# A feed-forward in a fixed order: the output weights' transfers take places further ahead in the transfer queue

## The chip, the cores and the metric

The kernel runs on one core of one Trainium2 chip. The metric is the device time of one execution in microseconds, median of several runs; the kernel before takes 1002.35 us (three runs: 1003.61, 1000.15 and 1002.35).

In the profile, PE is the matrix engine (TensorE) and PEld its weight loads, DVE is VectorE, ACT is ScalarE, POOL is GpSimd, and SP is the engine that issues nearly all transfers. Each of them takes its own instructions in order and waits at semaphores for the others.

## The reference

Two residual layers over a sequence of 512 frames of width 1024, in float32. Layer 0 mixes by pooling, layer 1 by chunked attention; each is followed by the same gated feed-forward with 2816 hidden channels, which is where the change lies:

```python
def conv_ffn(h, w_gate, w_val, conv_w, conv_b, w_out):
    a = h @ w_gate
    ap = jnp.pad(a, ((0, 0), (CONV_W - 1, 0), (0, 0)))
    a = ap[:, 0:S] * conv_w[0] + ap[:, 1:S + 1] * conv_w[1] + ap[:, 2:S + 2] * conv_w[2] + conv_b
    return (jax.nn.silu(a) * (h @ w_val)) @ w_out

for i in range(DEPTH):            # DEPTH = 2
    ...                           # pooling mixer or chunked attention, residual
    h = rmsnorm(x, ffn_norm[i])
    x = x + conv_ffn(h, ffn_w_gate[i], ffn_w_val[i], ffn_conv_w[i], ffn_conv_b[i], ffn_w_out[i])
```

## The kernel before

**Precision.** Every factor of a product is split in a high part and a low part (hi and lo), and a product is three matmuls: hi by hi, lo by hi, hi by lo (function `mm3`, lines 123 to 125). For a weight this means: a transfer brings the raw block, ACT copies it to hi with rounding (line 409), and DVE subtracts hi from raw to get lo (line 410). Tiles are named so in the trace: `wo_r` is a raw block of the out weights, `ow_h` and `ow_l` its two parts; `gv_r` is a raw block of the gate or value weights, `g_h` and `g_l` its parts.

**The hidden blocks.** The 2816 hidden channels are 22 blocks of 128 (f = 0 to 21). A block takes two raw weight blocks of 512 KB, gate and value. From block 5 on they go through seven smaller products with sums of weights (`sa`, `sb`) before them and sums of results behind them; from block 8 on, these are the "wide" form of lines 610 and 612, in the banks `st_m`, `st_b` and `st_t`. ACT copies the first state of the bank `st_m` to the tile `v` (line 619) before PE may go on into that bank. The steps of three neighbouring blocks are interleaved by a table written out by hand, `PLACES`, and from block 8 to the end of the table the order in which DVE, ACT and SP get their instructions is the order of the code. PE's order is that of the code throughout.

**The out product.** The 22 blocks form four groups of 5, 6, 6 and 5 (`OUT`). When a group's hidden blocks are finished, the generator `output(g)` works it into the residual stream: for each of 8 row blocks d of the result it needs the weights of (g, d), 320 or 384 KB, and makes one `mm3` for each hidden block of the group, which PE runs between the products of the next group's hidden blocks. The loop at the end of `ffn` pulls from the generator with `next(queue[0])`, one matmul at a time, at a rate worked out from `points`, `WAIT` and `HOLD`. So while the hidden blocks of group 1 are computed, PE works off the out product of group 0, and so on; that of group 3 comes alone at the end.

**Buffers of the out weights.** For groups 0 to 2 the raw block goes to a buffer of its own (`tag="or"`) in a pool with one buffer for each name, so the transfer of a row block can start only when DVE has made the lo part of the row block before it. The hi and lo parts have two buffers each. For group 3 the raw blocks share the three buffers of the gate and value weights.

**Order around the change.** `load(d + 1)` issues the transfer and, right behind it, the hi part at the start of row block d; the lo part follows two `mm3` later (line 810). SP issues transfers in the order of the code, and one that waits for its buffer holds up all behind it.

## Time and profile before

| | |
|---|---|
| runs | 1003.61, 1000.15, 1002.35 us; median 1002.35 us |
| the profiled execution | 1003.79 us, of which the span of its instructions is 1001.9 us |
| PE busy | 972.8 us, 97% of the span |
| DVE busy | 804.4 us, 80% |
| ACT busy | 572.5 us, 57% |
| POOL busy | 103.2 us, 10% |
| transfers | 102.83 MB, mean 103 GB/s |
| mean granted clock of PE | 0.994 |

Times in the profile count from the start of the span. The feed-forward of layer 0 lies at about 45 to 385 us, attention follows, and the feed-forward of layer 1 begins at about 640 us and ends the kernel. The part in which the order of DVE, ACT and SP is that of the code lies at about 131 to 345 us in layer 0 and 733 to 965 us in layer 1. A matmul's record is about 0.39 us long, but the next one starts 0.23 us after it: records of neighbours overlap. In a list of waits, "A <- B: x, n, y" says that A's engine sat idle for x us in total before A, n times, the longest y, until B. In a timeline the last bracket is the idle time before an instruction and what ended it.

### The profile page before, as it was taken

To read this page: it belongs to the slowest core of one execution; us is meant where nothing else is said; L and a number is where in the kernel's file an instruction comes from. 1 tells how busy PE (TensorE), PEld (TensorE's weight loads), DVE (VectorE), ACT (ScalarE), POOL (GpSimd) and SP (SyncE) were. 2 spreads that over 40 slices of the span, in tenths; PEclk is the share of its full clock that TensorE was granted. 3 is DMA by queue.
4 is the path that set the end of the run, shared out by engine and by line. 5 is a ranking of instruction groups with operands and counts; after the bars stand their busy time and mean duration, and the time that the engine had idled before them with its cause. 6 is when DMAs were issued, how large, how long until landed. Compare 5 with 4: busy or idle time off the path is not lost.

```text
span 1001.9 us, 13807 instructions
## 1 busy us (share of the span) xinstructions
PE 972.8 (97%) x5038; PEld 821.5 (82%) x5038; DVE 804.4 (80%) x1452; ACT 572.5 (57%) x990; POOL 103.2 (10%) x90
## 2 busy tenths in 40 slices
PE   9999999899989999999999999999999889989998
PEld 8788988788868888888888787888988778778886
DVE  8999889889879855442786888999989787889953
ACT  7665555546446444345898887565555444446521
POOL 2300000000000013204435441000000000000000
PEclk9999999999999999999999999999999999999999
DMA  8222232232223224232443342332322323232323
GB/s 332 92 76 86 90 111 94 93 115 75 85 106 116 71 82 146 88 122 85 123 117 93 91 119 75 100 110 70 112 91 75 116 74 101 89 116 74 101 83 112
DMA packets 37428, 102.83 MB, mean 103 GB/s; under 512 B 4432, under 2 KB 7904, under 8 KB 37360
## 3 DMA queue, kind: packets, MB, share of 16 engines
q1 hardware_dynamic: 37296, 101.90, 30.9%
q8 instruction: 40, 0.66, 0.3%
q14 instruction: 28, 0.23, 0.1%
q0 software_dynamic: 32, 0.04, 0.0%
q10 hardware_dynamic: 32, 0.00, 0.0%
HBM read 95.60 MB, written 2.14 MB: 98 GB/s over the span
## 4 chain that ended last, share of the span: by engine, by line
PE 64%; DVE 21%; DMA 7%; ACT 4%; issue 3%; SPq 0%; DVEq 0%; ACTq 0%
DMA wo_r<-wout 7%; PE out L124 5%; PE out L125 5%; PE out L123 5%; PE st_m L610 4%; PE gv L124 3%; PE gv L125 3%; PE gv L123 3%; PE qk L124 3%; PE qk L123 3%; PE qk L125 3%; DVE g_l L410 3%; PE st_m L612 2%; DVE ow_l L410 2%; PE st_t L610 2%
## 5 line engine op out<-in xcount | busy, mean ns | idle before, releaser
L409 ACT ACTIVATE ow_h<-wo_r 128x640 fp32r<-128x640 f32 (+1 forms) x64 | 50.6, 790 | 124.7 <-DMA wo_r<-wout 83.1
L125 PE MATMUL out<-one,ow_l 128*128 128x512 f32 x224 | 88.4, 395 | 3.6 <-DVE ow_l L410 3.6
L123 PE MATMUL out<-one,ow_h 128*128 128x512 f32 x224 | 88.5, 395 | 0.0
L124 PE MATMUL out<-one,ow_h 128*128 128x512 f32 x224 | 88.4, 395 | 0.0
L610 PE MATMUL st_m<-two,g_h 128*128 128x512 f32 x224 | 72.4, 405 | 14.6 <-ACT v L619 14.5
L817 DVE TENSOR_TENSOR X<-out,X 128x512 f32<-128x512 f32 (+1 forms) x65 | 43.9, 677 | 42.0 <-PE out L125 41.9
L610 PE MATMUL st_m<-h,g_h 128*128 128x512 f32 x224 | 70.5, 396 | 0.0
L610 PEld LDWEIGHTS st_m<-two,g_h 128*128 128x128 f32 x224 | 40.3, 189 | 28.7 <-ACT v L619 20.2
L424 DVE SCALAR_TENSOR_TENSOR c<-a,col,c 128x511 f32<-128x511 f32 (+1 forms) x76 | 56.1, 741 | 3.2 <-ACT c L421 3.2
L410 DVE TENSOR_TENSOR ow_l<-wo_r,ow_h 128x640 fp32r<-128x640 f32 (+1 forms) x64 | 56.4, 882 | 2.4 <-ACT ow_h L409 2.4
L125 PEld LDWEIGHTS out<-one,ow_l 128*128 128x128 f32 x224 | 42.5, 190 | 10.9 <-DVE ow_l L410 4.5
L125 PE MATMUL qk<-wqk_h,two 128*128 128x512 f32 x128 | 51.4, 402 | 0.0
L610 PEld LDWEIGHTS st_m<-h,g_h 128*128 128x128 f32 x224 | 42.8, 191 | 9.8
L123 PE MATMUL qk<-wqk_h,two 128*128 128x512 f32 x128 | 50.8, 409 | 0.0
L124 PE MATMUL qk<-wqk_l,two 128*128 128x512 f32 x128 | 50.8, 397 | 0.0
L612 PEld LDWEIGHTS st_m<-two,g_l 128*128 128x128 f32 x224 | 42.7, 191 | 9.4
L123 PEld LDWEIGHTS out<-one,ow_h 128*128 128x128 f32 x224 | 42.8, 191 | 6.1
L124 PEld LDWEIGHTS out<-one,ow_h 128*128 128x128 f32 x224 | 42.6, 190 | 6.3 <-DVE one L435 0.3
L1047 DVE CUSTOM_DVE_ANT_0 sb<-sc,B 128x128 f32<-128x128 f32 (+1 forms) x64 | 31.1, 485 | 18.9 <-PE sc L1044 18.1
L612 PE MATMUL st_m<-h,g_l 128*128 128x256 f32 x224 | 45.5, 285 | 0.0
L421 ACT ACTIVATE c<-a,col 128x512 f32<-128x512 f32 x38 | 30.6, 810 | 26.0 <-DVE a L768 24.6
L612 PE MATMUL st_m<-two,g_l 128*128 128x256 f32 x224 | 44.8, 282 | 0.0
(378 smaller groups left out, 2966.8 us busy)
## 6 DMA issues: line engine op xcount, KB each, us to landing
gv_r<-gv SPq DMA_DIRECT2D x86, 512.0 KB, 3.7
wo_r<-wout SPq DMA_DIRECT2D x32, 384.0 KB, 4.5
wo_r<-wout SPq DMA_DIRECT2D x32, 320.0 KB, 2.9
wqk_r<-wqk SPq DMA_DIRECT2D x16, 512.0 KB, 3.4
wv_r<-wv SPq DMA_DIRECT2D x8, 512.0 KB, 3.4
wo_r<-wo SPq DMA_DIRECT2D x8, 512.0 KB, 3.4
xt<-xt SPq DMA_DIRECT2D x4, 512.0 KB, 5.4
X<-xT SPq DMA_DIRECT2D x8, 256.0 KB, 7.5
```

What stands on the lines that cost most here:

```text
L123: yield nc.tensor.matmul(o, sh, mh, start=first, stop=False, **how)
L124: yield nc.tensor.matmul(o, sh, ml, start=False, stop=False, **how)
L125: yield nc.tensor.matmul(o, sl, mh, start=False, stop=last, **how)
L409: nc.scalar.activation(hi[:, :n], raw[:, :n], AF.Copy)
L410: return hi, lo, lambda: nc.vector.tensor_sub(lo[:, :n], raw[:, :n], hi[:, :n].bitcast(F32))
L421: nc.scalar.activation(c, a, AF.Identity, scale=cw[2], bias=cw[3])
L424: nc.vector.scalar_tensor_tensor(c[:, j:], a[:, :S - j], cw[2 - j], c[:, j:], op0=OP.mult, op1=OP.add)
L610: nc.tensor.matmul(o, hi[:, c], B[i, name], start=first and i == 0, stop=False, **how)
L612: nc.tensor.matmul(o[:, 0], lo[:, c], B[i, name][:, 0], start=False, stop=i == 3, **how)
L817: nc.vector.tensor_add(X[d][:, fs], o[:, fs], X[d][:, fs])
L1047: nc.vector.tensor_tensor_reduce(out=s_[:, :n], in0=sc[:, :n], in1=BT[h % 2][:, :n][:, ::-1], scale=1.0, scalar=3e38, op0=OP.add, op1=OP.m ...
```

## The change

Asking for a transfer and making the hi part are taken apart. `ask(g, d)` issues the transfer of (g, d), `halves(d)` makes its hi part. For groups 0 to 2, the transfer for row block d + 2 is now asked for right behind the lo part of row block d + 1, in the middle of row block d, and no longer at the start of row block d + 1. The first transfer of the next group is asked for in row block 6, behind the last lo part of the group (not for group 3). The generator has one more stop, behind the lo part of row block 0; the loop pulls it there at the second point of a group, so that this lo part and the transfer of row block 1 come ahead of the first matmul of the out product. For group 3, three transfers are asked for at once and then each behind a lo part.

```diff
+        asked = {}
+
+        def ask(g, d):
+
+            b, m = OUT[g]
+            asked[g, d] = raw_tile(f"wo{l}_{g}_{d}", wout[l, d, :, b * P:(b + m) * P], m * P, g + 1 < len(OUT))
+
         def output(g):
 
             b, m = OUT[g]
-            n = m * P
+            ahead = 1 if g + 1 < len(OUT) else 3
             w = []
 
-            def load(d):
-                w.append(parts(raw_tile(f"wo{l}_{g}_{d}", wout[l, d, :, b * P:(b + m) * P], n, g + 1 < len(OUT)), n, f"ow{l}_{g}_{d}", True, True))
-
-            load(0)
+            def halves(d):
+                w.append(parts(asked.pop((g, d)), m * P, f"ow{l}_{g}_{d}", True, True))
+
+            for d in range(ahead):
+                if (g, d) not in asked:
+                    ask(g, d)
+            halves(0)
             yield
             w[0][2]()
+            ask(g, ahead)
+            yield
             for d in range(KD):
                 if d + 1 < KD:
-                    load(d + 1)
+                    halves(d + 1)
                 o = psum("Q", f"out{l}_{g}_{d}")
                 for i in range(m):
                     if i == 2 and d + 1 < KD:
                         w[d + 1][2]()
+                        if d + 1 + ahead < KD:
+                            ask(g, d + 1 + ahead)
+                        elif d + 2 == KD and g + 2 < len(OUT):
+                            ask(g + 1, 0)
...
                     wait = WAIT[g]
+                    if g and at == 2:
+                        next(queue[0])
                     if at > wait:
...
                 left = KD * 3 * m
+            next(queue[0])
             run(queue.pop(0))
```

In the built programs the order of PE, ACT and POOL is the same before and after. On SP ten transfers of out weights in each layer stand further ahead, and on DVE two lo parts in each layer. The rows are the same in both layers. Nothing changes in the rows of group 3.

SP, layer 0, in hidden blocks 11 to 15 (`wo_1_3` is the transfer of group 1, row block 3; `gv_14_0` and `gv_14_1` are gate and value of hidden block 14), - before and + now:

```order
 L391 DMA gv_11_1_r<-gv 128x1024
+L391 DMA wo_1_0_r<-wout 128x768
 L391 DMA gv_12_0_r<-gv 128x1024
 L391 DMA gv_12_1_r<-gv 128x1024
-L391 DMA wo_1_0_r<-wout 128x768
+L391 DMA wo_1_1_r<-wout 128x768
 L391 DMA gv_13_0_r<-gv 128x1024
 L391 DMA gv_13_1_r<-gv 128x1024
-L391 DMA wo_1_1_r<-wout 128x768
 L391 DMA wo_1_2_r<-wout 128x768
+L391 DMA wo_1_3_r<-wout 128x768
 L391 DMA gv_14_0_r<-gv 128x1024
```

Each of the moved transfers passes one pair of gate and value transfers; `wo_1_2` keeps its place. So do `wo_0_7`, `wo_1_5`, `wo_2_2`, `wo_2_3` and `wo_2_5`; the ten that move are `wo_0_6`, `wo_1_0`, `wo_1_1`, `wo_1_3`, `wo_1_4`, `wo_1_6`, `wo_1_7`, `wo_2_0`, `wo_2_1` and `wo_2_4`.

DVE, layer 0, where the out product of group 1 is about to begin; before:

```order
L631 TENSOR_TENSOR v_1876<-v_1876 128x256
L651 TENSOR_TENSOR sb_1891<-gv_12_1_r 128x512
L786 TENSOR_TENSOR c_1836<-v_1742,c_1836 128x512
L655 TENSOR_TENSOR sa_1890<-sb_1891,gv_12_0_r 128x512
L625 TENSOR_TENSOR w_1902<-w_1902,st_11_t 128x512
L659 TENSOR_TENSOR sa_1890<-gv_12_0_r,gv_12_1_r 128x512
L631 TENSOR_TENSOR v_1876<-w_1902 128x256
L675 TENSOR_TENSOR sb_1891<-gv_12_0_r,sa_1890 128x512
L721 TENSOR_TENSOR g_11_l<-gv_11_1_r,g_11_h 128x512
L435 TENSOR_TENSOR one_95<-c_1836,one_87 128x512
L410 TENSOR_TENSOR ow_1_0_l<-wo_1_0_r,ow_1_0_h 128x768
```

and now:

```order
L410 TENSOR_TENSOR g_12_l<-gv_12_0_r,g_12_h 128x1024
L631 TENSOR_TENSOR v_1876<-v_1876 128x256
L410 TENSOR_TENSOR ow_1_0_l<-wo_1_0_r,ow_1_0_h 128x768
L651 TENSOR_TENSOR sb_1894<-gv_12_1_r 128x512
L786 TENSOR_TENSOR c_1838<-v_1744,c_1838 128x512
```

The lo part of (1, 0) has passed the nine instructions from `sb` to `one`. The same move is made for the lo part of (2, 0).

## The prediction

> **What bounds the kernel now.** I read the page first, then the list of waits by engine, then the timelines around the longest waits.

> ```profile
> span 1001.9 us, 13807 instructions
> PE 972.8 (97%) x5038; PEld 821.5 (82%) x5038; DVE 804.4 (80%) x1452; ACT 572.5 (57%) x990; POOL 103.2 (10%) x90
> DMA wo_r<-wout 7%; PE out L124 5%; PE out L125 5%; PE out L123 5%; PE st_m L610 4%; PE gv L124 3%; PE gv L125 3%; PE gv L123 3%; PE qk L124 3%; PE qk L123 3%; PE qk L125 3%; DVE g_l L410 3%; PE st_m L612 2%; DVE ow_l L410 2%; PE st_t L610 2%
> PE st_m L610 <- ACT v L619: 14.5, 12, 3.1
> PE out L125 <- DVE ow_l L410: 6.5, 4, 1.9
> ACT ow_h L409 <- DMA wo_r<-wout: 83.1, 24, 6.8
> ```

> PE is the bound, busy 972.8 of 1001.9 us, and nothing in this change makes its matmuls fewer. So only PE's idle time can be won. The chain of work that ended last nevertheless leads with the landing of out weights (7% of the span), and the list of waits says how: ACT sits 83.1 us before `ow_h`, and behind it in ACT's order stands the copy of `st_m` to `v`, for which PE waits 12 times, 14.5 us. Another four times, 6.5 us, PE waits for a lo part on DVE. These 16 waits make 21.0 us. All of them lie in the feed-forwards. One case, word for word, in layer 0:

> ```profile
> 202.98 0.95 DVE L410 TENSOR_TENSOR ow_l<-wo_r,ow_h 128x768 fp32r<-128x768 f32 x1
> 204.59 0.93 SPq L391 DMA_DIRECT2D gv_r<-gv  x2
> 205.62 0.38 SPq L391 DMA_DIRECT2D wo_r<-wout  x1
> 211.79 0.85 ACT L409 ACTIVATE ow_h<-wo_r 128x768 fp32r<-128x768 f32 x1 [3.74 <-DMA wo_r<-wout]
> 214.64 0.50 PE L610 MATMUL st_m<-two,g_h 128*128 128x512 f32 x1 [0.59 <-ACT v L619]
> ```

> The lo part of (1, 2) ends at 203.93 and frees the buffer, but SP has two gate and value transfers first. That of (1, 3) goes out at 205.62 behind 1 MB, and lands when ACT starts, 211.79. ACT had been ready at 208.05 (211.79 less 3.74). The 3.74 us pass through ACT to PE as 0.59.

> **What PE loses beyond the idle column.** Two things come on top.

> ```profile
> 184.43 0.39 PE L123 MATMUL out<-one,ow_h 128*128 128x512 f32 x1
> 184.66 0.40 PE L124 MATMUL out<-one,ow_h 128*128 128x512 f32 x1
> 186.92 0.50 PE L125 MATMUL out<-one,ow_l 128*128 128x512 f32 x1 [1.87 <-DVE ow_l L410]
> 187.26 0.39 PE L610 MATMUL st_b<-two,g_h 128*128 128x512 f32 x1
> 187.80:191.20 3.40, 3.40 (x12) 2.81 (x11) 0.20 (x1) 0.04 (x1) 0.00 (x0) 0.50 0.69 270
> 822.42 0.58 PE L610 MATMUL st_m<-two,g_h 128*128 128x512 f32 x1 [3.12 <-ACT v L619]
> 822.70:826.10 3.40, 3.40 (x11) 2.84 (x11) 3.22 (x6) 1.11 (x3) 0.00 (x0) 0.50 0.00 0
> 891.00:894.40 3.40, 3.40 (x12) 2.81 (x11) 2.52 (x6) 1.12 (x2) 0.00 (x0) 0.50 0.00 0
> ```

> Matmuls follow each other after 0.23 us (184.43 to 184.66), though a record is 0.39 long. Around the wait of 1.87 us the starts are 2.26 apart, 2.03 too many, and the next start comes after 0.34, another 0.11 too many. So a wait costs its idle time and some 0.27 us. And in three stretches of 3.4 us the granted clock is 0.50 (the number before the last two of a row by windows), each beginning just after a long wait: 3 × 3.4 × 0.5 = 5.1 us.

> **The change, part by part.** It adds and removes no instruction on PE, DVE or ACT, and no byte. It moves ten transfers in each layer past one pair of gate and value transfers, and two lo parts past nine DVE instructions.

> *The ten transfers.* The earliest start is the end of the lo part before (one raw buffer). Where does that leave the landing? Issued with nothing ahead of it, a transfer of this size takes 3.1 us:

> ```profile
> 230.77 0.33 SPq L391 DMA_DIRECT2D wo_r<-wout  x1
> DMA to landing us min/median/max: 3.1/3.1/3.1
> ```

> (the second row is for this one transfer). For (1, 3): 203.95 + 3.1 = 207.1, ahead of ACT's 208.05 by about 1 us. This is one of the tight kind, where the lo part just precedes the pair. Of the roomy kind is (1, 7):

> ```profile
> 248.28 0.95 DVE L410 TENSOR_TENSOR ow_l<-wo_r,ow_h 128x768 fp32r<-128x768 f32 x1
> 254.26 0.38 SPq L391 DMA_DIRECT2D wo_r<-wout  x1
> 259.60 0.85 ACT L409 ACTIVATE ow_h<-wo_r 128x768 fp32r<-128x768 f32 x1 [6.26 <-DMA wo_r<-wout]
> ```

> It can go at 249.2 instead of 254.26, so it lands at 252.4, and ACT is ready at 253.34. The wait of 6.26 us goes. SP gains no new stop: each moved transfer waits for a lo part that ends before the pair behind it could go (203.93 against 204.59; 249.2 against a pair that goes about 1 us before 254.26).

> *The two lo parts.* DVE makes that of (1, 0) at once after `v`:

> ```profile
> 177.27 0.85 ACT L409 ACTIVATE ow_h<-wo_r 128x768 fp32r<-128x768 f32 x1 [2.38 <-DMA wo_r<-wout]
> 180.77 0.68 DVE L651 TENSOR_TENSOR sb<-gv_r 128x512 f32<-128x512 f32 x1
> 185.92 0.95 DVE L410 TENSOR_TENSOR ow_l<-wo_r,ow_h 128x768 fp32r<-128x768 f32 x1
> 191.16 0.84 ACT L409 ACTIVATE ow_h<-wo_r 128x768 fp32r<-128x768 f32 x1 [6.21 <-DMA wo_r<-wout]
> ```

> It takes the place of `sb` at 180.77 and ends at 181.7; its hi part is there by 178.1. PE wants it at 184.9 (0.23 after 184.66), so the four waits for lo parts go. The transfer of (1, 1) leaves at 181.8 and lands at 184.9; ACT is ready for it at 184.95 (191.16 less 6.21), or later, since the nine passed DVE instructions come 0.9 us later. That delay is hidden by the 3 us by which PE is now early there, and by DVE's idle time soon after in the run before (up to 4.9 us; its row stands with the rivals). What is late next is bounded at 0.9 us for each of four places; I take 0, since the instructions passed feed products that PE reaches after `st_b`, later than 187.26.

> *What the moved transfers hold up.* Gate and value weights now stand behind 384 KB. At most places ACT finds them landed; in the whole run it waits for them five times, 1.5 us in all. The longest of these waits is at (1, 6), and (2, 4) is placed alike:

> ```profile
> ACT g_h L409 <- DMA gv_r<-gv: 1.5, 5, 0.5
> 242.00:244.00 2.00, 2.00 (x12) 1.75 (x11) 2.00 (x4) 1.21 (x2) 0.00 (x0) 1.00 1.00 388
> 243.61 1.06 ACT L409 ACTIVATE g_h<-gv_r 128x1024 fp32r<-128x1024 f32 x1 [0.52 <-DMA gv_r<-gv]
> 245.80 0.85 ACT L409 ACTIVATE ow_h<-wo_r 128x768 fp32r<-128x768 f32 x1 [0.61 <-DMA wo_r<-wout]
> 247.18 0.73 PE L610 MATMUL st_m<-two,g_h 128*128 128x512 f32 x2 [0.17 <-ACT v L619]
> 936.75 0.73 PE L610 MATMUL st_m<-two,g_h 128*128 128x512 f32 x2 [0.37 <-ACT v L619]
> ```

> At 388 GB/s, 384 KB (0.393 MB) take 1.0 us. ACT's wait for the gate weights of 0.52 becomes up to 1.5 while the 0.61 for the out weights goes: between a gain of 0.6 and a loss of 1.0 us at four places. The out transfer also starts about a microsecond earlier than the pair did, so I take no change, and leave the waits of 0.17 and 0.37 in.

> *The sum.* Lo parts 6.5; `v` 14.5 − 0.5 = 14.0; restarts 14 × 0.27 = 3.8; half clock 5.1: together 29.4 us. Something comes back. How much, the stretches without waits tell:

> ```profile
> 180.00:300.00 120.00, 111.75 (x565) 93.09 (x566) 99.69 (x160) 59.97 (x89) 0.00 (x0) 0.99 0.28 95
> 300.00:345.00 45.00, 45.00 (x235) 37.91 (x235) 43.05 (x72) 25.34 (x37) 0.00 (x0) 1.00 0.29 97
> 780.00:940.00 160.00, 148.20 (x752) 124.44 (x751) 136.32 (x219) 80.74 (x119) 0.00 (x0) 0.98 0.28 97
> 326.48 0.39 PE L123 MATMUL out<-u1h,ow_h 128*128 128x512 f32 x1
> 326.86 0.73 PE L610 MATMUL st_m<-two,g_h 128*128 128x512 f32 x2
> ```

> (columns: length, then PE, PEld, DVE, ACT, POOL busy.) From 300 to 345 us PE has no idle time although DVE is at 43.05 of 45, 96%; it shows two hitches, of which the row at 326.86 is the first: 0.15 ahead of it (0.38 from start to start instead of 0.23) and 0.11 inside it (0.73 for a pair that takes 0.62 undisturbed, 0.39 + 0.23). That is 0.53 us in 45. Over the 280 us in which the waits now lie this makes 3.3 us. Net 29.4 − 3.3 = 26.1 us. The profiled execution took 1003.79 us, 1.9 around its span, and would take 977.7; it stands 1.4 above the median of the runs, so the median goes from 1002.35 to 976.3.

> [...]

> **Rivals.**

> *DVE becomes the bound.* Without its waits PE needs about 160 − 11.8 idle − 1.9 for seven restarts − 3.4 for two half-clock stretches = 142.9 us from 780 to 940, and DVE has 136.3 busy there, 95%. For it: little is left for the bends of an order in which each waits for the other. Against it: the 96% of 300 to 345, with 0.53 us lost. DVE's idle time there is mostly ACT's doing:

> ```profile
> DVE a L768 <- ACT a L763: 17.4, 4, 4.9
> ```

> (780 to 940 us), of 23.7 idle; if the other 6.3 stays, DVE needs 142.6 and is level with PE. If half of the 26.1 us is lost in this way, the time is 989; with a quarter to five sixths lost it is 983 to 998.

> *The half clock stays* and has another cause than the waits: for it, that there are 16 waits and three stretches; against it, that the stretches of 187.8 and 822.7 begin 0.9 and 0.3 us after the end of a long wait. 976.3 + 5.1 = 981.4 us.

> *The transfers gain nothing.* The one buffer ties a transfer to the lo part before it; if the lo parts themselves come later because DVE falls behind, every landing comes as late as now. It needs a slip of more than 1 us at the tight places and 5 at the roomy ones. 1002 us.

> *Slower: the wait moves to the gate weights.* If each pair lands 1.0 us later and ACT stands for it before `g_h` at all 20 places, and PE takes all of it, while ACT's copies of `v` are as late as before, the time is 1002.35 + 20 = 1022; with the four tight places alone, 1006. It decides from the point at which the pair's slack falls under 1.0 us at most places; now it is under that at (1, 6) and (2, 4) only.

> **How the numbers follow.** Forecast (972 to 982): 0.70. Half clock stays: 0.06. DVE bound: 0.16. No gain: 0.04. Slower: 0.04. The likeliest gives 976.3. The least time is the sum without anything back, with the two small waits gone too: 1002.35 − 30.4 = 972. Upward the range takes in the half clock and the better half of the DVE case, to 987; outside lie about 0.06 of that case, the two last and a little below 972. A difference of 0.3% (3 us) is about what a measurement of this kernel tells from none: faster 0.92, same 0.04, slower 0.04.

> **What would show it.** Right: ACT's wait for out weights falls from 83.1 us to under 15; PE's waits for `v` and for lo parts fall from 21.0 to under 4; the three half-clock stretches are gone; the transfer of (1, 3) is issued ahead of its pair and lands in about 3 us; PE is busy above 99% from 180 to 300. Wrong: PE waits for `v` as long as before with ACT held by DVE or by `gv_r`, or DVE at 100% over a whole group with PE's idle time spread in front of products that read `g_l`.

## The result, and the profile after

The changed kernel takes 972.62 us (four runs, 972.58 to 972.73), the kernel before 1001.25 us (four runs, 998.95 to 1003.61): a ratio of 0.9714, 95% interval 0.9689 to 0.9739. The forecast was 976.3, in a range of 972 to 987. The profiled execution took 972.73 us.

The page of the changed kernel: span, busy time, and the chain of work that ended last, by engine and by line.

```profile
span 970.9 us, 13813 instructions
PE 962.8 (99%) x5038; PEld 819.1 (84%) x5038; DVE 804.9 (83%) x1452; ACT 575.4 (59%) x990; POOL 103.1 (11%) x90
PE 94%; DVE 4%; ACT 2%; issue 0%; DMA 0%; DVEq 0%; ACTq 0%
PE st_m L610 11%; PE out L124 8%; PE out L125 8%; PE out L123 8%; PE st_m L612 5%; PE st_t L610 5%; PE gv L124 4%; PE gv L125 4%; PE gv L123 4%; PE qk L124 3%; PE qk L123 3%; PE qk L125 3%; PE st_t L612 3%; PE st_b L610 3%; PE tp L1078 2%; PE oo L1090 2%
```

The landing of out weights, which led the chain with 7%, is gone from it; the chain is PE. DVE and ACT are busy for as long as before. The list of waits shows that nothing has taken the place of what went. All of PE's waits, then three of ACT's:

```profile
PE warm L205 <- POOL ident masks.py:199: 1.4, 1, 1.4
PE wo L124 <- DVE two L103: 0.7, 1, 0.7
PE oo L1090 <- DVE pt1l L103: 0.5, 1, 0.5
PE tp L1078 <- ACT sb L1070: 0.5, 2, 0.3
PE y L289 <- ACT two L228: 0.4, 1, 0.4
PE po L123 <- DVE one L108: 0.3, 1, 0.3
...
ACT ow_h L409 <- PE out L124: 46.5, 30, 3.3
ACT ow_h L409 <- DMA wo_r<-wout: 3.2, 2, 1.9
ACT g_h L409 <- DMA gv_r<-gv: 2.7, 9, 0.4
```

The rows `st_m <- v` (14.5 us) and `out <- ow_l` (6.5 us) do not stand there at all; what is left lies at the start and in the mixers. ACT's wait for out weights fell from 83.1 to 3.2 us; where ACT now stands before `ow_h`, it is ahead of PE, which still reads the buffer to be written. The price that the gate weights pay for standing behind 384 KB is 2.7 us of ACT's time in place of 1.5, in nine short waits.

Stretches of the fixed part (length; PE, PEld, DVE, ACT, POOL busy; then granted clock, share of the data engines, GB/s), in layer 0 and in layer 1:

```profile
180.00:300.00 120.00, 120.00 (x631) 102.79 (x630) 113.53 (x182) 68.88 (x99) 0.00 (x0) 1.00 0.33 107
766.00:926.00 160.00, 160.00 (x841) 136.75 (x840) 150.03 (x241) 90.25 (x132) 0.00 (x0) 1.00 0.31 101
```

PE has no idle time and full clock in both, with DVE at 95% and 94%. And the case of (1, 3), which the prediction read, in the timeline after:

```profile
198.56 0.95 DVE L410 TENSOR_TENSOR ow_l<-wo_r,ow_h 128x768 fp32r<-128x768 f32 x1
199.58 0.33 SPq L391 DMA_DIRECT2D wo_r<-wout  x1
200.15 0.93 SPq L391 DMA_DIRECT2D gv_r<-gv  x2
204.33 0.85 ACT L409 ACTIVATE ow_h<-wo_r 128x768 fp32r<-128x768 f32 x1 [0.69 <-PE out L124]
206.55 0.58 ACT L619 ACTIVATE v<-st_m 128x512 f32<-128x512 f32 x1
209.22 0.62 PE L610 MATMUL st_m<-two,g_h 128*128 128x512 f32 x2
```

The transfer leaves 0.07 us after the lo part frees the buffer (199.51), the pair behind it 0.57 us later. ACT waits for PE and not for the landing, and the copy to `v` ends at 207.13, 2.1 us before PE goes on in that bank.

### The profile page after: what moved, and what is told of

Read it like the earlier page. It is cut to its first block, busy times and chain, and to the rows that moved or that the text cites. A ratio compares the mean times of both kernels' runs of the same rounds, so it can differ in the third digit from the quotient of the medians.

```text
span 970.9 us, 13813 instructions
## 1 busy us (share of the span) xinstructions
PE 962.8 (99%) x5038; PEld 819.1 (84%) x5038; DVE 804.9 (83%) x1452; ACT 575.4 (59%) x990; POOL 103.1 (11%) x90
## 2 busy tenths in 40 slices
DMA packets 37428, 102.83 MB, mean 106 GB/s; under 512 B 4432, under 2 KB 7904, under 8 KB 37360
## 3 DMA queue, kind: packets, MB, share of 16 engines
q1 hardware_dynamic: 37296, 101.90, 32.4%
## 4 chain that ended last, share of the span: by engine, by line
PE 94%; DVE 4%; ACT 2%; issue 0%; DMA 0%; DVEq 0%; ACTq 0%
PE st_m L610 11%; PE out L124 8%; PE out L125 8%; PE out L123 8%; PE st_m L612 5%; PE st_t L610 5%; PE gv L124 4%; PE gv L125 4%; PE gv L123 4%; PE qk L124 3%; PE qk L123 3%; PE qk L125 3%; PE st_t L612 3%; PE st_b L610 3%; PE tp L1078 2%; PE oo L1090 2%
## 5 line engine op out<-in xcount | busy, mean ns | idle before, releaser
L124 PE MATMUL out<-one,ow_h 128*128 128x512 f32 x224 | 88.0, 393 | 0.0
L123 PE MATMUL out<-one,ow_h 128*128 128x512 f32 x224 | 87.8, 392 | 0.0
L125 PE MATMUL out<-one,ow_l 128*128 128x512 f32 x224 | 87.8, 392 | 0.0
L409 ACT ACTIVATE ow_h<-wo_r 128x640 fp32r<-128x640 f32 (+1 forms) x64 | 50.4, 787 | 55.0 <-PE out L124 46.5
L610 PE MATMUL st_m<-two,g_h 128*128 128x512 f32 x224 | 70.0, 394 | 0.0
L610 PE MATMUL st_m<-h,g_h 128*128 128x512 f32 x224 | 69.1, 389 | 0.0
L410 DVE TENSOR_TENSOR ow_l<-wo_r,ow_h 128x640 fp32r<-128x640 f32 (+1 forms) x64 | 56.8, 888 | 2.5 <-ACT ow_h L409 2.5
L125 PE MATMUL qk<-wqk_h,two 128*128 128x512 f32 x128 | 51.4, 402 | 0.0
L123 PE MATMUL qk<-wqk_h,two 128*128 128x512 f32 x128 | 50.8, 409 | 0.0
L124 PE MATMUL qk<-wqk_l,two 128*128 128x512 f32 x128 | 50.8, 397 | 0.0
L610 PEld LDWEIGHTS st_m<-h,g_h 128*128 128x128 f32 x224 | 42.1, 188 | 9.6
L619 ACT ACTIVATE w<-st_m 128x512 f32<-128x512 f32 x28 | 16.7, 598 | 56.0 <-PE st_m L612 56.0
L612 PEld LDWEIGHTS st_m<-two,g_l 128*128 128x128 f32 x224 | 42.0, 188 | 8.8
L610 PEld LDWEIGHTS st_m<-two,g_h 128*128 128x128 f32 x224 | 41.1, 188 | 9.3 <-ACT w L619 0.8
L124 PEld LDWEIGHTS out<-one,ow_h 128*128 128x128 f32 x224 | 42.3, 189 | 6.3 <-DVE one L435 0.3
L125 PEld LDWEIGHTS out<-one,ow_l 128*128 128x128 f32 x224 | 42.3, 189 | 6.3
L123 PEld LDWEIGHTS out<-one,ow_h 128*128 128x128 f32 x224 | 42.3, 189 | 6.0
L612 PE MATMUL st_m<-h,g_l 128*128 128x256 f32 x224 | 45.1, 283 | 0.0
```

The source lines that it names most:

```text
L123: yield nc.tensor.matmul(o, sh, mh, start=first, stop=False, **how)
L124: yield nc.tensor.matmul(o, sh, ml, start=False, stop=False, **how)
L125: yield nc.tensor.matmul(o, sl, mh, start=False, stop=last, **how)
L409: nc.scalar.activation(hi[:, :n], raw[:, :n], AF.Copy)
L410: return hi, lo, lambda: nc.vector.tensor_sub(lo[:, :n], raw[:, :n], hi[:, :n].bitcast(F32))
L610: nc.tensor.matmul(o, hi[:, c], B[i, name], start=first and i == 0, stop=False, **how)
```

## The experiments

The theory was that two places decide: that of a transfer in SP's order, which makes ACT late before the copy to `v`, and that of the first lo part on DVE, which makes PE wait by itself. The rivals were that one cause makes all waits, that the single raw buffer holds the transfers up, that transfers are slow beside others, and that only waits at certain places reach PE. The kernel before gave 999.68, 999.66 and 999.20 us (medians) beside the three groups of runs below, against 1001.25 beside the change itself. The change was not run again in these groups, so a difference of 1 or 2 us from its 972.62 is not settled by the times alone; the waits in the profiles are the better evidence for it. In each of these kernels the order of PE and ACT is that of the changed kernel.

**The transfers alone, without the early lo parts**

```diff
@@ the changed kernel, output(g) and the loop
             w[0][2]()
             ask(g, ahead)
-            yield
...
-                    if g and at == 2:
-                        next(queue[0])
...
-            next(queue[0])
             run(queue.pop(0))
```

> The change without its early lo parts: eight of the ten transfers of each layer stand ahead as in the change; the lo parts of (1, 0) and (2, 0), and with them the transfers of (1, 1) and (2, 1), stand where they stood before. Theory (the place in SP's order makes ACT late, the place of the lo part makes PE wait by itself): PE's waits for `v` go except the one of 0.76 us behind (2, 1), and the four waits for lo parts stay, 6.5 us in all, with 0.27 for each restart and one or two half-clock stretches: 972.6 + 6.5 + 1.1 + 2 x 1.0 + 1.7 to 3.4 = 982 to 985.5 us. Rival (the waits for lo parts were themselves late through ACT's waits, and go with those): under 976 us.

Measured: 992.75 us, ratio 0.9921 (0.9893 to 0.9948). That is 20 us above the change and outside of both expectations. In the profile (timeline and list of waits):

```profile
184.28 0.40 PE L124 MATMUL out<-one,ow_h 128*128 128x512 f32 x1
186.46 0.95 DVE L410 TENSOR_TENSOR ow_l<-wo_r,ow_h 128x768 fp32r<-128x768 f32 x1
187.46 0.80 PE L125 MATMUL out<-one,ow_l 128*128 128x512 f32 x1 [2.79 <-DVE ow_l L410]
...
PE out L125 <- DVE ow_l L410: 11.2, 4, 2.8
```

The wait for `v` is gone completely, as the theory said. But the four waits for lo parts grew from 6.5 to 11.2 us: DVE makes the lo part no earlier than before, and PE, no longer held up on the way there, comes sooner and stands longer. This run's times stand 0.54 us later than those of the kernel before already ahead of the changed part (the same matmul at 165.91 and 165.37). With that taken off, the lo part starts at 185.92 as before, and PE starts the matmul ahead of the wait at 183.74 and not at 184.66: 0.92 sooner, which is what the wait grew by (1.87 to 2.79). Behind the wait shown the granted clock is 0.50 for 6.8 us, from 186.70 to 193.50; over the whole span it is 0.991, against 0.999 in the change, and 0.008 of 991.0 us is some 7.9 us (the clock is known to 0.001, so to 1 us or so). 11.2 + 1.1 for restarts + 7.9 = 20.2, against a span longer by 20.1 than the change's.

**The early lo parts alone**

```diff
@@ the kernel before, output(g) and the loop
             load(0)
             yield
             w[0][2]()
+            yield
...
+                    if g and at == 2:
+                        next(queue[0])
                     if at > wait:
...
+            next(queue[0])
             run(queue.pop(0))
```

> Only the early lo parts of (1, 0) and (2, 0); every transfer stands where it stood before. Theory: the four waits for lo parts go (6.5 us, four restarts 1.1, one half-clock stretch 1.7), the waits for `v` stay (about 14 us): 1001.3 - 9.3 = 992 us, with 2 us either way. Rival (the delay that ACT's landings make is the one cause of all): no change, 999 to 1002 us.

Measured: 1003.29 us, ratio 1.0040 (1.0024 to 1.0057): no gain, a small loss, and outside of both expectations. The waits for lo parts are gone, and now those for `v` have grown:

```profile
192.34 0.85 ACT L409 ACTIVATE ow_h<-wo_r 128x768 fp32r<-128x768 f32 x1 [5.74 <-DMA wo_r<-wout]
197.11 0.73 PE L610 MATMUL st_m<-two,g_h 128*128 128x512 f32 x2 [1.94 <-ACT v L619]
...
PE st_m L610 <- ACT v L619: 19.3, 13, 3.1
```

At this matmul (197.88 in the kernel before) PE did not wait before the change: it had stood 1.87 us and run at half clock ten us earlier. The lo part's wait hid the lateness of the transfer of (1, 1) behind it. The loss of 3.6 us cannot be read from the two lists of waits, since the profile of the kernel before is of an execution of 1003.79 us, above the medians of that kernel: its waits make 21.0 us, these 19.3. The granted clock fits the loss: 0.991 to 0.994 in the six executions of this run, 0.995 to 0.998 in the nine of the kernel before beside it, and 0.004 (the medians, 0.993 and 0.997) of 1000 us is 4 us. So each part of the change alone gives 7 us or less, and both give 28.6.

**The queue instead of the order: out weights asked for by GpSimd**

```diff
@@ the kernel before, raw_tile
-            nc.sync.dma_start(raw[:, :n], src)
+            (nc.gpsimd if own else nc.sync).dma_start(raw[:, :n], src)
```

> The kernel before, with the out weights of groups 0 to 2 asked for by GpSimd, which has nothing else to do in the feed-forwards, in place of SP. The one raw buffer and the order of the lo parts are as before, the order of all other engines too. Theory (a transfer waits in SP's queue behind a pair): each leaves when its lo part frees the buffer; PE's waits for `v` go as in the run of the asks alone, the waits for lo parts stay: 980 to 987 us. Rival one (the single buffer ties the transfer): nothing changes, 999 to 1002 us. Rival two (the transfer is slow because it shares the data engines with the pair): it still lands 4.5 us or more after issue at most places and half of the waits for `v` stay: 990 to 997 us.

Measured: 992.40 us, ratio 0.9922 (0.9899 to 0.9945), the same as that of the transfers alone. That is above the 980 to 987 of the theory and within the range of rival two, but not by that rival's way: under it half of the waits for `v` stay, and none is left. Nothing was moved in the code, and the one raw buffer stayed; the queue in which a transfer waits for its buffer holds no pair any more. From the queues, the page and the list of waits:

```profile
q0 software_dynamic: 3872, 17.87, 6.1%
wo_r<-wout POOLq DMA_DIRECT2D x32, 384.0 KB, 3.4
...
PE out L125 <- DVE ow_l L410: 11.1, 4, 2.8
```

A transfer lands 3.4 us after issue (median; 4.5 before, 3.1 in the change), and the four waits for lo parts are again 2.8 us each. This rules out the buffer and leaves SP's order. GpSimd's transfers also go by a queue of another kind (q0 in the first row, where 101.90 of the 102.83 MB of the kernel before go by `q1 hardware_dynamic`), so this run alone does not part the order from the kind of queue; the run of the transfers alone, in SP's queue, does, with the same time. It says nothing against sharing as such: that transfers land sooner because they no longer leave together with a pair is the likely reason, and was not tested apart.

**Both, with that queue**

```diff
@@ the run of the early lo parts alone, raw_tile
-            nc.sync.dma_start(raw[:, :n], src)
+            (nc.gpsimd if own else nc.sync).dma_start(raw[:, :n], src)
```

> The kernel before with the early lo parts of (1, 0) and (2, 0), and with the out weights of groups 0 to 2 asked for by GpSimd at their old places in the code. No transfer is reordered in the code, but none stands behind a gate and value pair any more. Theory (what counts is that a transfer can leave when its lo part has freed the buffer, and that the first lo part is early; either alone moves the wait): as fast as the change, 972 to 975 us, although the run of the GpSimd queue alone gave 992.4 and that of the lo parts alone 1003.3. Rival (the gain needs the transfers' order against the pairs at the data engines): 980 us or more.

Measured: 973.21 us, ratio 0.9738 (0.9719 to 0.9757). The two edits that gave 992.4 and 1003.3 alone give together what the change gives, to 0.6 us. That neither part counts for much without the other is so shown twice, by two different means of letting a transfer go.

**The second transfers of a group put back**

```diff
@@ the changed kernel, output(g); (g, d) in LATE is asked for in halves(d), where it stood before
+        LATE = ((1, 1), (2, 1))
...
             def halves(d):
+                if (g, d) not in asked:
+                    ask(g, d)
                 w.append(...)
...
             w[0][2]()
-            ask(g, ahead)
+            if (g, ahead) not in LATE:
+                ask(g, ahead)
...
                         if d + 1 + ahead < KD:
-                            ask(g, d + 1 + ahead)
+                            if (g, d + 1 + ahead) not in LATE:
+                                ask(g, d + 1 + ahead)
```

> The change, with the transfers of (1, 1) and (2, 1) alone put back behind their gate and value pair; the early lo parts of (1, 0) and (2, 0) stay. Theory (each part alone only moves the wait: with the early lo part, PE comes sooner to the copy to `v` that stands behind the hi part of row block 1, and that part has its transfer late): ACT waits some 5 us for each of the four, PE waits 2 to 3 us for `v` four times, each with a half-clock stretch: 972.6 + 10 + 1.1 + 6.8 = 990 us, with 3 us either way. Rival (the early lo part is worth its own 9 us whatever the transfer behind it does): 975 us or less.

Measured: 995.37 us (ten runs, 994.49 to 997.31), ratio 0.9953 (0.9936 to 0.9969), 2.4 us above the range expected and far from the rival. Two transfers in each layer are worth 22.8 us of the 28.6:

```profile
180.91 0.95 DVE L410 TENSOR_TENSOR ow_l<-wo_r,ow_h 128x768 fp32r<-128x768 f32 x1
186.85 0.42 SPq L391 DMA_DIRECT2D wo_r<-wout  x1
192.06 0.84 ACT L409 ACTIVATE ow_h<-wo_r 128x768 fp32r<-128x768 f32 x1 [6.10 <-DMA wo_r<-wout]
196.83 1.22 PE L610 MATMUL st_m<-two,g_h 128*128 128x512 f32 x2 [3.27 <-ACT v L619]
...
PE st_m L610 <- ACT v L619: 13.8, 4, 3.8
```

The lo part of (1, 0) ends at 181.9 here, and the transfer still leaves at 186.85. In the change it leaves at 181.76, and ACT makes the hi part at 185.70 without waiting. Four waits, 3.1 to 3.8 us each, with half clock for 6.8 us behind the one shown (0.50 from 195.60 to 202.40); the mean granted clock is 0.990.

**The other transfers put back**, by the same edit with another list:

| put back in each layer | measured | above the change |
|---|---|---|
| (1, 3) | 973.97 us, ratio 0.9746 (0.9724 to 0.9767) | 1.4 |
| (1, 3), (1, 6), (2, 4) | 974.55 us, ratio 0.9739 (0.9708 to 0.9770) | 1.9 |
| (0, 6), (1, 4), (1, 7) | 975.73 us, ratio 0.9748 (0.9712 to 0.9784) | 3.1 |
| all six | 979.52 us, ratio 0.9788 (0.9757 to 0.9820) | 6.9 |

Of (1, 3) alone:

> The change, with one transfer of each layer, that of (1, 3), put back behind its gate and value pair. Theory: it leaves at about 201.2 instead of 199.58 us and lands after some 6.1 to 6.8 us, so ACT starts its hi part at 207.3 to 208.0 instead of 204.33. The copy to `v` has 2.1 us to spare (it ends at 207.13, PE goes on at 209.22), so PE waits 0.9 to 1.6 us in each layer and pays 0.27 for the restart; no half-clock stretch follows: 972.6 + 2.3 to 3.7 = 975 to 976.5 us. Rival (the waits reach PE only where several follow each other): 972.6 us.

Only layer 0 had a wait, of 0.69 us; the landing took 6.0 us there and 4.9 in layer 1, where it stayed inside the slack of 2.1. So 1.4 us in the place of 2.3 to 3.7, and the slack read from the trace is about right. Of the three tight places:

> The change, with the transfers of (1, 3), (1, 6) and (2, 4) put back behind their pairs, the places at which the transfer can go only 1 to 2 us earlier. Theory: (1, 3) costs what it cost alone, 1.35 us for both layers; at (1, 6) and (2, 4) the wait for the out weights takes the place of that for the gate weights, and PE sees 0 to 0.4 us each: 974 to 976 us. Rival (gate weights behind 384 KB cost as much as the change gives there): 973 us or less at (1, 6) and (2, 4), that is 974 us with (1, 3).

0.6 us more than (1, 3) alone, with overlapping runs (973.97 to 975.80 against 973.77 to 974.66): (1, 6) and (2, 4) are worth little or nothing, as both expected, and the runs do not decide between them. Of the three roomy places:

> The change, with the transfers of (0, 6), (1, 4) and (1, 7) put back behind their pairs, where ACT stood 3 to 6 us before the change. Theory: ACT waits again some 3 to 6 us at each, of which PE sees what goes beyond its slack there, 0.5 to 1.3 us, too short for a half-clock stretch: 972.6 + 6 x 0.9 + 6 x 0.27 = 979 us, with 2 us either way. Rival (waits that do not stand at the beginning of a group are swallowed): 973 us.

3.1 us, half of what was expected, and between the theory's range and the rival. ACT waits 34.8 us for out weights in this run, and PE sees 1.5 of them, in three waits. Of all six:

> Of the change, only what stands at the beginning of groups 1 and 2: the early lo parts of row block 0 and the transfers of (1, 0), (1, 1), (2, 0) and (2, 1); the other six transfers of each layer stand as before the change. Theory (the beginning of a group is where the waits meet): the sum of the two runs that put back the rest, 972.6 + 6.5 + 2 = 981 us, with 3 us either way. Rival (one late transfer anywhere lets ACT fall behind and the waits at the beginning of the groups return): 990 us or more.

6.9 us, as expected within its 3 us, but 1.9 more than the 1.9 + 3.1 of the two runs before. In the profiled execution, whose span is 6.0 us longer than the change's, PE waits 3.3 us in five waits, with restarts 4.7; of the rest 0.4 us lie at the start, ahead of the changed part. ACT waits 45.7 us, 16 times:

```profile
PE st_m L610 <- ACT v L619: 3.3, 5, 1.0
ACT ow_h L409 <- DMA wo_r<-wout: 45.7, 16, 7.0
```

Against the run of the second transfers this is the plainest comparison of the study. There ACT waits 27.0 us for out weights and PE loses 22.8; here ACT waits 45.7 and PE loses 6.9. How long ACT waits says little; where it waits decides.

## Why the prediction was right, point by point

**What bounds the kernel.** Right. PE is now busy for 962.8 of 970.9 us. The 10.0 us less of busy time than before are for the most part the 5.1 of half clock and the 4.3 of restarts, which lie in records of PE and not in its idle time.

**The ten transfers.** Right: (1, 3) leaves at 199.58, ahead of its pair, and is no longer what ACT waits for; SP gained no stop that matters (its waits for `ow_l` and for the `sb` of line 675 make 455.7 us together, 484.9 before).

**The lo parts.** Right in what happens to the four waits and in the landing of (1, 1) (181.76 plus 3.1 is 184.9, ACT takes it up at 185.70). The nine instructions that were passed cost nothing, as taken: PE has no idle time from 180 to 300 us.

**The gate weights behind 384 KB.** Right in size: 1.2 us more of ACT's time in the whole run, none of it PE's. The two waits of 0.17 and 0.37 us that I left in went too.

**The sum.** The span fell by 31.0 us. The losses that were counted, 21.0 of idle time, 16 × 0.27 = 4.3 for restarts, and 5.1 of half clock, make 30.4, and all of them went. The term that was mis-sized is what comes back: I took 3.3 us at the rate of the stretch from 300 to 345 us. After the change one hitch of 0.26 is left in the fixed part of each layer, here in layer 0 (0.38 from start to start, 0.73 for the pair). The first three rows are after the change, PE's and one of ACT; the last is the same matmul before it:

```profile
330.49 0.39 PE L124 MATMUL out<-u3l,ow_h 128*128 128x512 f32 x1
330.87 0.73 PE L610 MATMUL st_m<-two,g_h 128*128 128x512 f32 x2
330.22 0.60 ACT L619 ACTIVATE w<-st_m 128x512 f32<-128x512 f32 x1 [2.94 <-PE st_m L612]
...
344.06 0.73 PE L610 MATMUL st_m<-two,g_h 128*128 128x512 f32 x2
```

This hitch stood there before the change too, as one of the two that I had counted (and at 953.90 in layer 1); the other, at 326.86, went. So nothing came back in the place of the 3.3 us, and one hitch of 0.26 went besides. This hitch kept its place in the order, behind a copy out of the bank `st_m` (that to `w`, which ends at 330.82, 0.05 us before PE goes on), and a rate by time, carried over to other places, was no measure of it.

Part of the miss is hidden by luck. The profiled execution was to go from 1003.79 to 977.7 us, and that of the change took 972.73: 5.0 us less, of which 3.3 are this term and 1.0 the two small waits that I had left in, with their restarts. Between 976.3 and 972.62 lie only 3.7, because I took off another 1.4 us, by which the profiled execution stood above the median; that of the change stands 0.1 above its own.

**What the sum left unseen.** I priced the lo parts and the transfers as terms that add. They do not: in the runs of one part, the wait moved to the other and became longer (11.2 us in the place of 6.5, 19.3 in the place of 14.5). The forecast came out right because the change makes both; the same sum for one of them, 982 to 985.5 and 992, missed by 7 and 11 us.

**The rivals.** DVE did not become the bound, though it is at 95% of the fixed part. The half clock did go with the waits, which speaks for its cause in them, against the 981.4 of the rival. Neither "no gain" nor the slower case came.

## What to carry to other kernels

In this kernel a transfer of out weights that stood behind a pair in SP's order was held until that pair could leave, whatever its own buffer did: that of (1, 1) left at 186.85 us behind a pair of 185.87, 5 us after its own buffer fell free at 181.9, and with two such transfers put back in each layer the time was 995.37 us in place of 972.62. What to try elsewhere is to ask for a transfer where its buffer falls free, ahead of transfers that need their data later (972.62 us), or from a queue that has nothing else in it (973.21). PE waited here at two places that follow each other closely, and each wait hid the other: mending one gave 992.75 us or 1003.29, the second of which looks like a loss, and the trial that told was both together. The length of a helper engine's wait was no measure of what it cost (45.7 us of ACT's for 6.9 us in one run, 27.0 for 22.8 in another); read the slack in front of the bounding engine's next use of its result.

## What the runs showed of the hardware

```profile
884.40:887.80 3.40, 1.88 (x13) 1.50 (x11) 2.95 (x6) 2.26 (x4) 0.00 (x0) 1.00 0.13 52
887.80:891.20 3.40, 2.82 (x16) 2.48 (x17) 3.40 (x6) 1.82 (x5) 0.00 (x0) 1.00 0.00 0
802.50:805.90 3.40, 1.63 (x9) 1.20 (x8) 3.40 (x7) 1.97 (x4) 0.00 (x0) 1.00 0.39 116
805.90:809.30 3.40, 3.40 (x11) 2.73 (x10) 3.40 (x7) 2.20 (x4) 0.00 (x0) 0.50 0.00 0
```

Behind the stretch with 1.88 us of PE's time busy (1.52 idle) the next one ran at full clock; behind that with 1.63 (1.77 idle), at 0.50. The length of the wait alone did not tell. In the kernel before, the wait of 1.87 us that ends at 186.92 lay in one step, and the stretch behind it lost 1.7 us (half of 3.4); that of 2.04 us that ends at 280.85 lay across two steps, 1.16 us in one and 0.88 in the other, and both they and the next ran at full clock. That the division is the reason is read from these places alone; no run shifted a wait to try it. In the run of the transfers alone, a stretch that was itself at half clock, with 0.76 us idle (the second row here), had another at half clock behind it:

```profile
183.30:186.70 3.40, 1.37 (x8) 0.86 (x6) 3.40 (x7) 1.50 (x2) 0.00 (x0) 1.00 0.11 19
186.70:190.10 3.40, 2.64 (x7) 2.16 (x8) 1.84 (x2) 0.00 (x0) 0.00 (x0) 0.50 0.97 373
190.10:193.50 3.40, 3.40 (x11) 2.82 (x10) 1.05 (x2) 2.20 (x4) 0.00 (x0) 0.50 0.08 32
```

The kernel before scatters (997.2 to 1004.5 us over all its runs) and the changed one hardly does (972.58 to 972.73). The half clock explains that only in small part. The granted clock is known for 29 executions of the kernel before, 0.993 to 1.000, and it goes with the time only weakly: the fastest, of 997.20 us, had 0.994, one with 1.000 took 999.20, and the slowest, of 1004.49, had 0.993. In the run of the transfers alone the two do go together: 988.19 us at 0.998, and 992.67 to 992.90 at 0.991 and 0.992. What else makes the kernel before scatter is not shown.
